# The low-rank gate product stacked in f32r, another pace for the gated linear attention, and a last product that is token-major

## The chip, the cores and the metric

One core of a Trainium2 chip runs the whole program in one launch. The metric is the device time of one execution in microseconds (us), the median of several runs. Before the change it is 1217.9 us (3 runs, 1216.07 to 1218.35).

## What is computed

Two blocks on one sequence of 512 tokens with 1024 features. The first is a hybrid mixer (pooling, two convolutions, differential attention) with a feed-forward net. The second puts 16 meta tokens in front (528 tokens in all) and has two layers, "ab" and "cd". Layer ab has eight heads of sparse attention (an indexer scores all keys, the 128 best are kept) and four heads of gated linear attention (GLA). Layer cd has four heads of retention and eight heads of stick-breaking attention, an output product, the residual sum and a last norm. The change touches the GLA of layer ab and the end of layer cd:

```python
log_a = log_sigmoid(ba @ gate_w2 + gate_b) / 16       # ba: 16 columns per token, gate_w2: 16 x 256
bcum = cumsum(log_a, within chunks of 64 tokens)
q_t, k_t = q * exp(bcum), k * exp(-bcum)              # then chunked linear attention with a carried state
...
h = h + concat([oc, od]) @ w_out_cd                   # end of layer cd
return h[16:] * rsqrt(mean(h[16:]**2) + 1e-6) * final_g
```

All inputs and outputs are float32.

## The kernel before

**Layout.** Activations lie feature-major: `self.x[kt]` holds features 128 kt to 128 kt + 127 on the partitions and tokens along the free axis. A large product is made of three f32r products: each operand is split into a rounded part (`hhi`, `whi`) and the rest (`hlo`, `wlo`), and hi*hi, lo*hi and hi*lo are added in PSUM (`f_acc`, its matmul is L154). Weights come as one stream in the order of use: `weights` (L129) loads a unit of 512 KB into one of two `wraw` tiles on SP's queue, ScalarE rounds it (L139) and VectorE makes the rest (L140), into four `whi` and four `wlo` tiles.

**Order.** The program is written as foreground projections, and `f_acc` calls `tick` after each pair of weight blocks: 8 ticks in a projection over 528 tokens (48 matmuls). One tick advances the generator at the head of the list `bg` by one `yield`. `pipe` runs a staged piece of work as such a generator: one round of stages, then `pace` yields. `finish(x)` ticks until x is done. On top of this the Tile framework places each engine's instructions by priority and by its own model of time: `first()` raises the priority, `chain()` raises it most. On the chip each engine works its list strictly in that order.

**Layer ab.** After the indexer's four query projections comes a projection `bw` of 104 columns: 64 indexer keys, 16 columns `ba` (partitions 64 to 79), 8 indexer weights. Then `score` (L855, L856) and `choose` (16 rounds of MAX8 and MATCH_REPLACE8 per block of 128 queries, L873 and L874, on VectorE; the masks `mk` are L876) stand in the list of generators while `bqk` and `bv` are projected. Then `gla` sets up its factors in a `chain()` block: the gate product (L1064, plain fp32, 16 rows, `gw2` as stationary and `bw[64:80]` as moving operand), Abs (L1065), min (L1066), Exp and Ln, the scan over time (L1071) with a tile `reset` of ones and zeros, and exponentials and products up to L1092. `reset` is one of the two `tmp` tiles, loaded at this point by SP (L1058). `linear` then runs five items (16 meta tokens, four blocks of 128) through four stages at a pace of 4, with fp32 matmuls (L1146, L1149, L1169, L1171, L1124). After it stand the projections of `av` (4) and those of `dsa_cols(0)` (q, k, gate); `finish(gla)` follows, then the output gates of GLA and the sparse attention `dsa` (L982 to L1032), whose blocks need the masks `mk`.

**End of layer cd.** When all heads are done, the `od` part is split into `mixed` (L112, L113) and the last four weight units are kept. For each half of the tokens (256 columns) 8 output tiles are made by `add_out`: 12 f32r matmuls of 256 columns, the residual sum on VectorE (L304), square on ScalarE (L242, L245), sum of squares on VectorE (L247), the product with `final_g` on ScalarE (L1378). Then `norm` sums over partitions with fp32 matmuls (L262), makes the inverse root (L264, L212 to L219), spreads it over partitions by two more matmuls (L223) and a copy (L269); eight multiplications (L1385) and four DMAs (L1386) end the half. The output is feature-major and is transposed on the host.

`transpose` (L184) is a fp32 matmul against the identity.

Of the kernel before, what the change touches and what calls it, by code (L numbers as in the profile page):

```python
# [18 lines left out]
S = 512  # L19
M = 16  # L20
T = S + M
H2 = M + S // 2
D = 1024
# [24 lines left out]
COLS, NCOLS = _names((("g1", 8), ("g2", 8), ("ga", 8), ("gc", 8), ("gf", 8), ("pscale", 2), ("sconv", 6),  # L48
# [12 lines left out]
class Kern:  # L61
    def __init__(self, ctx, tc, io, dbg=None):
        self.tc, self.nc, self.io = tc, tc.nc, io
        self.dbg = dbg or {}
        E = ctx.enter_context
        self.hot = E(tc.tile_pool(name="hot", bufs=1))

        self.hot.tile([128, 32], F32, name="pad1")
        self.wp = E(tc.tile_pool(name="w", bufs=2))
        self.const = E(tc.tile_pool(name="const", bufs=1))  # L70
        self.big = E(tc.tile_pool(name="big", bufs=1))
        self.dram = E(tc.tile_pool(name="dram", bufs=1, space=DRAM))
        self.big.tile([128, 24], F32, name="pad2")
# [746 lines left out]
    def layer_ab(self, act, acc):  # L820
# [4 lines left out]
        with tc.tile_pool(name="ab", bufs=1, reuse_waits="tile") as p:  # L825
            F4 = lambda n, w=T: p.tile([128, 4, w], F32, name=n)
            gw2 = p.tile([128, 256], F32, name="gw2")[64:80]
            nc.sync.dma_start(gw2, self.io["gw2"])
# [70 lines left out]
            gla = self.gla(p, bqk, bv, bvm, bw, gw2)  # L899
# [152 lines left out]
    def gla(self, p, bqk, bv, bvm, bw, gw2):  # L1052
# [3 lines left out]
        with self.chain():  # L1056
            reset = self.tmp(p)
            nc.sync.dma_start(reset, self.io["csa"][:, CSA["reset"][0]:CSA["reset"][0] + T])  # L1058
            for f in range(2):
                gb = self.cols[:, COLS["gb"][0] + f:COLS["gb"][0] + f + 1]  # L1060
                t, t2 = ks2[:, f], eb[:, f]
                for k0, k1 in ALL:
                    ps = self.ch("a")[:, :k1 - k0]
                    nc.tensor.matmul(ps, lhsT=gw2[:, f * 128:f * 128 + 128], rhs=bw[64:80, k0:k1], start=True, stop=True)  # L1064
                    nc.scalar.activation(t[:, k0:k1], ps, AF.Abs, bias=gb)  # L1065
                    nc.vector.tensor_scalar(t2[:, k0:k1], ps, gb, 0.0, op0=OP.add, op1=OP.min)  # L1066
# [30 lines left out]
            def masked(a, ps, n, e):  # L1097
# [3 lines left out]
                        lambda t: att0[t % 2], masked, bqk, True)  # L1101

    def linear(self, p, q, k, kx, qs, ks, v, vm, decay, att, masked, out, meta):
# [93 lines left out]
        yield from self.pipe([scores, attend, norm, finish], items, 4)  # L1197
# [75 lines left out]
    def layer_cd(self, act, acc):  # L1273
# [3 lines left out]
        with tc.tile_pool(name="cd", bufs=1, reuse_waits="tile") as p:  # L1277
# [35 lines left out]
            with self.chain():  # L1313
# [35 lines left out]
                def masked(a, ps, n, e):  # L1349
# [3 lines left out]
                            lambda t: p.tile([128, 4, 128], F32, name="att", bufs=2), masked, cqk, False)  # L1353
# [15 lines left out]
            acc = self.newacc()  # L1369

            self.keep = True
            ws = [self.weights(4, 256) for _ in range(4)]
            for c0 in (M, M + 256):
                c = slice(c0, c0 + 256)

                def after(kt):
                    self.sumsq(kt, c0, c0 + 256, acc, nc.vector)
                    nc.scalar.mul(self.x[kt][:, c], self.x[kt][:, c], self.cols[:, COLS["gf"][0] + kt:COLS["gf"][0] + kt + 1])  # L1378

                self.add_out(mixed, ((c0, c0 + 256),), after, ws)  # L1380
                _, rb = self.norm(acc, False, (c0, c0 + 256))
                for i, (k0, k1) in enumerate(((0, 2), (2, 4), (4, 6), (6, 8))):
                    for kt in range(k0, k1):
                        x = self.x[kt][:, c]
                        nc.vector.tensor_tensor(out=x, in0=x, in1=rb[:, c], op=OP.mult)  # L1385
                    (nc.sync if i % 2 else nc.scalar).dma_start(self.io["out"][k0:k1].rearrange("k p t -> p k t")[:, :, c0 - M:c0 - M + 256], self.xs[:, k0:k1, c])  # L1386
# [101 lines left out]
def _arrays(a):  # L1488
# [11 lines left out]
    for n, v in (("g1", a["norm1_g"][0]), ("g2", a["norm2_g"][0]), ("ga", a["norm_g_2"][0]), ("gc", a["norm_g_2"][1]),  # L1500
                 ("gf", a["final_g_2"]), ("pscale", a["pool_scale"][0]), ("sconv", a["sconv_w"][0].T),
                 ("cw", a["conf_dw_w"][0].T), ("cb", a["conf_dw_b"][0]), ("lng", a["conf_ln_g"][0]),
                 ("lnb", a["conf_ln_b"][0]), ("gb", a["gla_gate_b_2"][0]), ("sub", np.tile(a["subln_g"][0], 2))):
        col(n, v)
    out["cols"] = cols
    out["rows"] = np.concatenate([a[n][0] for n in ("q_norm_g", "k_norm_g", "lam_q1", "lam_k1", "lam_q2", "lam_k2")])
    out["relb"] = np.concatenate([a["rel_bias"][ORDER1].T, a["rel_bias_2"][ORDER2].T], axis=0)
# [16 lines left out]
    def wout(w, k0, k1):  # L1524
        for c in range(0, D, 256):
            unit(w, k0, k1, c, c + 256)
# [51 lines left out]
    wout(a["w_out_cd_2"][0], 4, 8)  # L1578
# [4 lines left out]
_OUT = (KT, 128, S)  # L1583
# [15 lines left out]
```

## Time and profile before

| | us |
|---|---|
| median of 3 runs | 1217.9 (1216.07 to 1218.35) |
| the profiled execution | 1222.06 |
| its span, first to last instruction | 1220.3 |
| TensorE busy (PE) | 1195.1 (98%) |
| VectorE busy (DVE) | 809.1 (66%) |
| ScalarE busy (ACT) | 622.0 (51%) |
| mean granted TensorE clock | 0.991 |

A timeline row reads: start, duration, engine, line, operation, output tile, input tiles, partitions x elements, count, and in brackets the idle time of the engine before it with what ended it. The duration of a matmul includes its way through the array, so matmuls overlap in the rows; how fast they pass is read from the distance of two starts. PEld is the load of a stationary operand, SPq and ACTq are DMA issues. The granted clock is 1.00 at 2.4 GHz and 0.50 at 1.2 GHz.

### The profile page before, as it was taken

How to read it: one execution, taken by the hardware profiler on the slowest of the kernel's cores; microseconds unless marked ns; L12 is line 12 of the kernel's file. 1: busy time of each engine (PE TensorE's matmuls, PEld its weight loads, DVE VectorE, ACT ScalarE, POOL GpSimd, SP SyncE). 2: the span in 40 equal slices, each digit the busy share in tenths (PEclk: the TensorE clock that was granted, in tenths of full speed). 3: DMA queues.
4: the chain of work that ended last, by engine and by line, in shares of the span. 5: the costliest groups of instructions: out<-in, count | busy, mean ns of one | idle time of the engine just before them, and what ended most of it. 6: DMA issues, size and time to landing. Idle time of an engine off the chain costs nothing.

```text
span 1220.3 us, 18958 instructions
## 1 busy us (share of the span) xinstructions
PE 1195.1 (98%) x7234; PEld 1022.5 (84%) x7234; DVE 809.1 (66%) x1834; ACT 622.0 (51%) x1382; POOL 51.1 (4%) x77
## 2 busy tenths in 40 slices
PE   8989899999999999999999999999999999999996
PEld 6978788888888888888999899898899889876776
DVE  6899966444433444455799899666575576775775
ACT  6378656333323333344453345656563575575754
POOL 7000002000000000011000000000020000000000
PEclk9999999999999999999999999999999999999998
DMA  7422123223223332234221122222132213220122
GB/s 235 114 70 70 37 68 104 89 101 101 74 95 113 101 102 88 84 96 127 73 70 61 36 78 79 71 71 64 59 103 91 87 53 105 70 70 18 52 69 70
DMA packets 33308, 101.28 MB, mean 83 GB/s; under 512 B 4048, under 2 KB 6640, under 8 KB 33216
## 3 DMA queue, kind: packets, MB, share of 16 engines
q1 hardware_dynamic: 30528, 95.66, 24.6%
q0 software_dynamic: 880, 2.25, 0.7%
q10 hardware_dynamic: 1808, 2.16, 0.5%
q8 instruction: 57, 0.93, 0.3%
q14 instruction: 35, 0.29, 0.1%
HBM read 95.87 MB, written 3.10 MB: 81 GB/s over the span
## 4 chain that ended last, share of the span: by engine, by line
PE 86%; DVE 9%; ACT 3%; DMA 1%; issue 1%; SPq 0%; DVEq 0%; ACTq 0%
PE mm L154 68%; PE psb L184 3%; DVE wlo L140 2%; DVE y L605 2%; PE pso L1265 1%; DMA wraw<-in_w 1%; DVE sc L874 1%; PE pso L1018 1%; DVE m L873 1%; ACT whi L139 1%; PE psa L1146 1%; PE pso L1020 1%; PE pso L566 1%; PE mm L173 1%; DVE qk L749 1%
## 5 line engine op out<-in xcount | busy, mean ns | idle before, releaser
L154 PE MATMUL mm<-hhi,whi 128*128 128x512 f32 (+2 forms) x1280 | 432.8, 338 | 0.0
L154 PE MATMUL mm<-hlo,whi 128*128 128x512 f32 (+2 forms) x1280 | 427.5, 334 | 0.0
L154 PE MATMUL mm<-hhi,wlo 128*128 128x512 f32 (+2 forms) x1280 | 427.0, 334 | 0.0
L139 ACT CAST whi<-wraw 128x512 fp32r<-128x512 f32 x350 | 207.6, 595 | 328.4 <-PE mm L154 297.1
L140 DVE TENSOR_TENSOR wlo<-wraw,whi 128x512 fp32r<-128x512 f32 x350 | 233.9, 672 | 153.5 <-ACT whi L139 127.4
L154 PEld LDWEIGHTS mm<-hhi,whi 128*128 128x128 f32 x1280 | 242.4, 189 | 23.9 <-issue 2.2
L154 PEld LDWEIGHTS mm<-hlo,whi 128*128 128x128 f32 x1280 | 242.3, 189 | 21.8 <-issue 0.8
L154 PEld LDWEIGHTS mm<-hhi,wlo 128*128 128x128 f32 x1280 | 242.1, 189 | 21.8
L154 PE MATMUL mm<-mx,whi 128*128 128x512 f32 (+2 forms) x448 | 113.5, 342 | 3.5 <-ACT mx L112 3.3
L154 PEld LDWEIGHTS mm<-mx,whi 128*128 128x128 f32 x448 | 76.7, 192 | 15.7 <-ACT mx L112 4.1
L710 DVE TENSOR_TENSOR gu<-mm,rb 128x512 f32<-128x512 f32 x44 | 30.4, 691 | 68.8 <-PE mm L154 67.0
L154 PE MATMUL mm<-mx,wlo 128*128 128x512 f32 (+2 forms) x224 | 75.0, 335 | 0.0
L154 PE MATMUL mm<-hidh,wlo 128*128 128x512 f32 x176 | 68.5, 389 | 0.0
L154 PE MATMUL mm<-hidh,whi 128*128 128x512 f32 x176 | 68.5, 389 | 0.0
L154 PE MATMUL mm<-hidl,whi 128*128 128x512 f32 x176 | 68.5, 389 | 0.0
L247 POOL TENSOR_TENSOR acc<-acc,sq 128x528 f32<-128x528 f32 (+1 forms) x18 | 25.7, 1426 | 806.6 <-ACT sq L245 489.5
L316 DVE TENSOR_TENSOR tmp<-mm,rb 128x272 f32<-128x272 f32 (+2 forms) x76 | 35.6, 468 | 24.0 <-PE mm L154 22.8
L304 DVE TENSOR_TENSOR x<-x,mm 128x272 f32<-128x272 f32 (+2 forms) x72 | 36.7, 509 | 14.4 <-PE mm L154 13.2
L154 PEld LDWEIGHTS mm<-mx,wlo 128*128 128x128 f32 x224 | 42.8, 191 | 3.6
L605 DVE SCALAR_TENSOR_TENSOR y<-u,cols,y 128x512 f32<-128x512 f32 x60 | 42.5, 747 | 0.2
L154 PEld LDWEIGHTS mm<-hidh,wlo 128*128 128x128 f32 x176 | 33.0, 188 | 6.9
L154 PEld LDWEIGHTS mm<-hidh,whi 128*128 128x128 f32 x176 | 33.0, 188 | 6.9
(406 smaller groups left out, 1819.6 us busy)
## 6 DMA issues: line engine op xcount, KB each, us to landing
wraw<-in_w SPq DMA_DIRECT2D x145, 512.0 KB, 3.5
wraw<-in_w SPq DMA_DIRECT2D x16, 384.0 KB, 2.9
wraw<-in_w SPq DMA_DIRECT2D x16, 320.0 KB, 2.8
bh<-tab SPq DMA_DIRECT2D x16, 132.0 KB, 2.9
mx<-cqk SPq DMA_DIRECT2D x8, 132.0 KB, 2.4
x<-in_x SPq DMA_DIRECT2D x4, 256.0 KB, 7.3
x<-in_x ACTq DMA_DIRECT2D x4, 256.0 KB, 4.6
B<-tab POOLq DMA_DIRECT2D x4, 256.0 KB, 8.2
```

The source lines that it names most:

```text
L139: self.nc.scalar.copy(hi[:, :w], raw[:, c])
L140: self.lo.tensor_tensor(out=lo[:, :w], in0=raw[:, c], in1=hi[:, :w].bitcast(F32), op=OP.subtract)
L154: nc.tensor.matmul(ps[b], lhsT=ww[i][:, f0:f0 + nf], rhs=aa[:, t0:t1], start=first and i == 0 and j == 0, stop=last and i == n - 1 and j == 2)
L173: nc.tensor.matmul(part(t), lhsT=aa[:, t0:t0 + nt], rhs=ww[i], start=u + i + j == 0 and t % 2 == 0, stop=u == 1 and i == 3 and j == 2, ski ...
L184: self.nc.tensor.transpose(out, in_, self.ident[:n, :n])
L247: e.tensor_tensor(out=acc[:, c0:c1], in0=acc[:, c0:c1], in1=sq[:, c0:c1], op=OP.add)
L304: nc.vector.tensor_tensor(out=x, in0=x, in1=p, op=OP.add)
L316: self.nc.vector.tensor_tensor(out=out[:, t0:t1], in0=p, in1=rb[:nf, t0:t1], op=OP.mult)
L566: nc.tensor.matmul(o[:, h * 64:h * 64 + 64], lhsT=pT[:, j * 128:(j + 1) * 128], rhs=vt[:, j, h * 64:h * 64 + 64], start=j == 0, stop=j == i)
L605: nc.vector.scalar_tensor_tensor(y[:, f], u[:, f, k:k + S], cw[:, f, k:k + 1], y[:, f], op0=OP.mult, op1=OP.add)
L710: nc.vector.tensor_tensor(out=t[:, g], in0=ps, in1=rbx, op=OP.mult)
L749: nc.vector.tensor_tensor(out=ll[a:a + 64], in0=src, in1=hh[r:r + 64].bitcast(F32), op=OP.subtract)
```

## The change

1. The gate product is stacked: a tile `bs` of 80 rows holds the rounded `ba` on rows 0 to 15 and 64 to 79 and the rest on rows 32 to 47 (zeros between), `gw2` holds the rounded weights on rows 0 to 15 and 32 to 47 and their rest on rows 64 to 79. One f32r matmul with 80 rows gives the three partial products. `bs` takes a `qk` slot, the raw weights a `tmp` slot.
2. `reset` is a tile of its own, loaded at the start of layer ab.
3. `linear` runs GLA at a pace of 6; retention keeps 4.
4. The last product is token-major: for each block of 128 tokens and each half of the features, four transposes put the residual into a PSUM bank, and 12 f32r matmuls of 512 columns add to it. The square sum comes from ScalarE's `accum_out`, `final_g` is a row spread over partitions by DMA (`gf`, two `tmp` tiles), the inverse root is a column, and each half is stored by one DMA. The last four weight units have shape 2 x 512 in place of 4 x 256. `final_g` leaves the `cols` table (8 columns), and a pad tile grows by 8 columns.

```diff
-            gw2 = p.tile([128, 256], F32, name="gw2")[64:80]
-            nc.sync.dma_start(gw2, self.io["gw2"])
+            gw2 = p.tile([128, 256], F32R, name="gw2")[:80]
+            reset = p.tile([128, T], F32, name="reset")
+            nc.sync.dma_start(reset, self.io["csa"][:, CSA["reset"][0]:CSA["reset"][0] + T])
...
+            bs = p.tile([128, T], F32R, name="qk", bufs=self.nqk)[:80]
+            graw = self.tmp(p)[:80, :256]
+            with self.chain():
+                nc.gpsimd.memset(graw, 0.0)
+                for r in (0, 32, 64):
+                    nc.sync.dma_start(graw[r:r + 16], self.io["gw2"])
+                nc.scalar.copy(gw2, graw)
+                nc.vector.tensor_tensor(out=gw2[64:80], in0=graw[64:80], in1=gw2[64:80].bitcast(F32), op=OP.subtract)
+                nc.gpsimd.memset(bs.bitcast(F32), 0.0)
+                for r in (0, 64):
+                    nc.scalar.copy(bs[r:r + 16], bw[64:80])
+                nc.vector.tensor_tensor(out=bs[32:48], in0=bw[64:80], in1=bs[64:80].bitcast(F32), op=OP.subtract)
...
-            reset = self.tmp(p)
-            nc.sync.dma_start(reset, self.io["csa"][:, CSA["reset"][0]:CSA["reset"][0] + T])
...
-                    nc.tensor.matmul(ps, lhsT=gw2[:, f * 128:f * 128 + 128], rhs=bw[64:80, k0:k1], start=True, stop=True)
+                    nc.tensor.matmul(ps, lhsT=gw2[:, f * 128:f * 128 + 128], rhs=bs[:, k0:k1], start=True, stop=True)
...
-        yield from self.pipe([scores, attend, norm, finish], items, 4)
+        yield from self.pipe([scores, attend, norm, finish], items, pace)
...
-            ws = [self.weights(4, 256) for _ in range(4)]
-            for c0 in (M, M + 256):
-                c = slice(c0, c0 + 256)
-
-                def after(kt):
-                    self.sumsq(kt, c0, c0 + 256, acc, nc.vector)
-                    nc.scalar.mul(self.x[kt][:, c], self.x[kt][:, c], self.cols[:, COLS["gf"][0] + kt:COLS["gf"][0] + kt + 1])
-
-                self.add_out(mixed, ((c0, c0 + 256),), after, ws)
-                _, rb = self.norm(acc, False, (c0, c0 + 256))
-                for i, (k0, k1) in enumerate(((0, 2), (2, 4), (4, 6), (6, 8))):
-                    for kt in range(k0, k1):
-                        x = self.x[kt][:, c]
-                        nc.vector.tensor_tensor(out=x, in0=x, in1=rb[:, c], op=OP.mult)
-                    (nc.sync if i % 2 else nc.scalar).dma_start(...)
+            ws = [self.weights(2, 512) for _ in range(4)]
+            for t in range(4):
+                c = slice(M + 128 * t, M + 128 * t + 128)
+                ps = [self.ch("a") if t % 2 else self.mm() for _ in range(2)]
+                ss = p.tile([128, 2], F32, name="ss", bufs=2)
+                out = []
+                for half in range(2):
+                    for j in range(4):
+                        nc.tensor.matmul(ps[half][:, j * 128:(j + 1) * 128], lhsT=self.x[half * 4 + j][:, c], rhs=self.ident,
+                                         is_transpose=True, start=j == 0, stop=False, skip_group_check=True)
+                    for k in range(4):
+                        ah, al = mixed[k]
+                        wh, wl = (w[k % 2] for w in ws[half * 2 + k // 2])
+                        for j, (aa, ww) in enumerate(((ah, wh), (al, wh), (ah, wl))):
+                            nc.tensor.matmul(ps[half], lhsT=aa[:, c], rhs=ww[:, :512], start=False, stop=k == 3 and j == 2, skip_group_check=True)
+                    with self.first():
+                        sq = self.big.tile([128, T], F32, name="sq")
+                        nc.scalar.activation(sq[:, :512], ps[half], AF.Square, accum_out=ss[:, half:half + 1])
+                        out.append(p.tile([128, S], F32, name="L", bufs=5))
+                        if half == 0:
+                            nc.vector.tensor_scalar(ss[:, 0:1], ss[:, 0:1], 1.0 / D, EPS, op0=OP.mult, op1=OP.add)
+                            nc.vector.tensor_tensor(out=out[0], in0=ps[0], in1=gf[0], op=OP.mult)
+                with self.first():
+                    nc.vector.scalar_tensor_tensor(ss[:, 0:1], ss[:, 1:2], 1.0 / D, ss[:, 0:1], op0=OP.mult, op1=OP.add)
+                    self.rsqrt(ss[:, 1:2], ss[:, 0:1])
+                    nc.scalar.mul(out[0], out[0], ss[:, 1:2])
+                    nc.vector.scalar_tensor_tensor(out[1], ps[1], ss[:, 1:2], gf[1], op0=OP.mult, op1=OP.mult)
+                    for half, e in enumerate((nc.scalar, nc.sync)):
+                        e.dma_start(self.io["out"][t * 128:(t + 1) * 128, half * 512:(half + 1) * 512], out[half])
```

## Rows read from the trace of the kernel before

**Rows 1.** The page: busy time of each engine, and the chain that ended last by engine.

```profile
PE 1195.1 (98%) x7234; PEld 1022.5 (84%) x7234; DVE 809.1 (66%) x1834; ACT 622.0 (51%) x1382; POOL 51.1 (4%) x77
PE 86%; DVE 9%; ACT 3%; DMA 1%; issue 1%; SPq 0%; DVEq 0%; ACTq 0%
```

**Rows 2.** Timeline of PE alone around the gate product (L1064; each product leaves two records).

```profile
633.43 0.72 PE L1064 MATMUL psa<-qk,gw 16*128 16x272 f32 x2
634.08 0.38 PE L856 MATMUL psa<-qk 128*128 128x256 f32 x1
...
635.14 1.41 PE L1064 MATMUL psa<-qk,gw 16*128 16x256 f32 x4
636.48 0.39 PE L154 MATMUL mm<-hhi,whi 128*128 128x272 f32 x1
...
637.54 0.69 PE L1064 MATMUL psa<-qk,gw 16*128 16x256 f32 x2
638.16 0.54 PE L154 MATMUL mm<-hlo,whi 128*128 128x272 f32 x1
...
641.62 0.31 PE L154 MATMUL mm<-hlo,whi 128*128 128x256 f32 x1
```

**Rows 3.** Stretches of one us: PE, PEld, DVE, ACT and POOL busy (count of instructions), granted clock, DMA share, GB/s.

```profile
637.00:638.00 1.00, 1.00 (x7) 0.69 (x6) 0.90 (x3) 0.93 (x3) 0.00 (x0) 1.00 0.80 307
...
639.00:640.00 1.00, 1.00 (x6) 1.00 (x6) 0.28 (x1) 0.97 (x2) 0.00 (x0) 0.50 0.00 0
```

**Rows 4.** Timelines of SP, DVE and PE: the load of `reset`, the scan, the wait of PE for the end of the set-up; and DVE's longest idle time in this stage.

```profile
657.55 0.33 SPq L1058 DMA_DIRECT2D tmp<-in_csa x1
660.94 2.38 DVE L1071 TENSOR_TENSOR_SCAN mx<-tmp,mx 128x528 f32<-128x528 f32 x2
668.53 0.28 PE L184 MATMUL psb<-keep,mx 128*16 128x128 f32 x1 [1.03 <-ACT mx L1092]
641.01 0.44 DVE L316 TENSOR_TENSOR tmp<-mm,rb 128x272 f32<-128x272 f32 x1 [1.72 <-PE mm L154]
```

**Rows 5.** Stretches of 20 us, columns as in rows 3.

```profile
580.00:600.00 20.00, 20.00 (x137) 18.15 (x136) 11.96 (x22) 8.74 (x18) 0.00 (x0) 1.00 0.24 80
...
640.00:660.00 20.00, 19.62 (x155) 19.03 (x154) 18.17 (x56) 5.97 (x11) 0.00 (x0) 0.96 0.23 68
660.00:680.00 20.00, 18.97 (x171) 16.70 (x169) 18.63 (x48) 9.67 (x24) 0.00 (x0) 1.00 0.16 53
680.00:700.00 20.00, 20.00 (x166) 16.82 (x163) 17.26 (x57) 6.44 (x19) 0.00 (x0) 1.00 0.09 27
700.00:720.00 20.00, 20.00 (x163) 19.23 (x162) 18.97 (x54) 7.94 (x17) 0.00 (x0) 1.00 0.25 78
720.00:740.00 20.00, 18.82 (x151) 17.92 (x149) 19.85 (x49) 12.60 (x30) 0.00 (x0) 1.00 0.25 80
```

**Rows 6.** Groups by line and shape: count, busy us, mean ns, idle before.

```profile
L749 DVE TENSOR_TENSOR qk<-tmp,qk 64x528 fp32r<-64x528 f32 x32 | 22.4, 701 | 0.4
L540 ACT ACTIVATE e<-e,st 128x512 f32<-128x512 f32 x8 | 5.7, 718 | 0.0
L540 ACT ACTIVATION_READ_ACCUMULATOR e<-e,st 128x1 f32 x32 | 6.1, 190 | 0.0
L1095 POOL MEMSET att<- 128x512 f32 x2 | 1.0, 524 | 0.0
```

**Rows 7.** What SP's queue waited for: total us, times, longest; and the issue of the output's DMAs.

```profile
SPq L129 <- DVE wlo L140: 866.8, 153, 27.4
out<-x SPq DMA_DIRECT2D x4, 256.0 KB, 2.6
```

**Rows 8.** Timeline of PE: matmuls of 512 and of 256 columns, and groups of transposes between f32r matmuls.

```profile
1178.27 0.39 PE L154 MATMUL mm<-mx,wlo 128*128 128x512 f32 x1
...
1178.95 0.39 PE L154 MATMUL mm<-mx,wlo 128*128 128x512 f32 x1
...
1188.22 0.28 PE L154 MATMUL mm<-mx,hlo 128*128 128x256 f32 x1
...
1188.57 0.28 PE L154 MATMUL mm<-mx,hlo 128*128 128x256 f32 x1
...
658.09 0.79 PE L184 MATMUL psb<-keep,tmp 128*128 128x128 f32 x4
...
658.85 0.29 PE L154 MATMUL mm<-hhi,whi 128*128 128x272 f32 x1
...
696.63 0.60 PE L184 MATMUL psb<-keep,ot 128*128 128x128 f32 x4
...
697.18 0.28 PE L154 MATMUL mm<-hhi,wlo 128*128 128x256 f32 x1
```

**Rows 9.** Timeline of all engines at the end, from the first matmul of the last product.

```profile
1185.30 0.45 PE L154 MATMUL mm<-mx,hhi 128*128 128x256 f32 x2
...
1209.14 0.28 PE L154 MATMUL mm<-mx,hlo 128*128 128x256 f32 x1
...
1211.55 0.16 DVE L264 TENSOR_SCALAR rcv<-pso 128x2 f32<-128x2 f32 x1 [0.76 <-PE pso L262]
...
1212.60 0.16 DVE L219 SCALAR_TENSOR_TENSOR rc<-rt,ry 128x2 f32<-128x2 f32 x1
...
1213.94 2.77 DVE L1385 TENSOR_TENSOR x<-x,rb 128x256 f32<-128x256 f32 x8 [1.18 <-ACT rb L269]
```

More of the change, by code (lines that the diff above doesn't have):

```diff
@@ L72, in __init__ @@
         self.dram = E(tc.tile_pool(name="dram", bufs=1, space=DRAM))
-        self.big.tile([128, 24], F32, name="pad2")
+        self.big.tile([128, 32], F32, name="pad2")
         self.ps = E(tc.tile_pool(name="ps", bufs=1, space=PSUM))
@@ L898, in layer_ab @@
             self.finish(chosen)
-            gla = self.gla(p, bqk, bv, bvm, bw, gw2)
+            gla = self.gla(p, bqk, bv, bvm, bs, gw2, reset)
             self.bg.append(gla)
@@ L1050, in pipe, with gla @@
                 yield
-    def gla(self, p, bqk, bv, bvm, bw, gw2):
+    def gla(self, p, bqk, bv, bvm, bs, gw2, reset):
         nc = self.nc
@@ L1100, in gla, with linear @@
             return self.linear(p, bqk[:, 0:2], bqk[:, 2:4], ks, q2, ks2, bv, bvm, lambda f, t: dec[:, f, t:t + 1],
-                        lambda t: att0[t % 2], masked, bqk, True)
-    def linear(self, p, q, k, kx, qs, ks, v, vm, decay, att, masked, out, meta):
+                        lambda t: att0[t % 2], masked, bqk, True, 6)
+    def linear(self, p, q, k, kx, qs, ks, v, vm, decay, att, masked, out, meta, pace):
         nc = self.nc
@@ L1352, in layer_cd @@
                 ret = self.linear(p, cqk[:, 0:2], cqk[:, 2:4], None, qs, ks, cv, cvm, lambda f, t: dec[:, f:f + 1],
-                            lambda t: p.tile([128, 4, 128], F32, name="att", bufs=2), masked, cqk, False)
+                            lambda t: p.tile([128, 4, 128], F32, name="att", bufs=2), masked, cqk, False, 4)
             self.bg.append(ret)
@@ new lines, in layer_cd @@
+            for half in range(2):
+                gf.append(self.tmp(p)[:, :512])
+                g = self.io["gfr"]
+                nc.sync.dma_start(gf[half], bass.AP(tensor=g.tensor, offset=g.offset + half * 512, ap=[[0, 128], [1, 512]]))
+            self.keep = True
+            ws = [self.weights(2, 512) for _ in range(4)]
[4 more added lines that the diff above has]
+                out = []
+                for half in range(2):
+                    for j in range(4):
[20 more added lines that the diff above has]
+                        e.dma_start(self.io["out"][t * 128:(t + 1) * 128, half * 512:(half + 1) * 512], out[half])
@@ L1506, in _arrays @@
     out["rows"] = np.concatenate([a[n][0] for n in ("q_norm_g", "k_norm_g", "lam_q1", "lam_k1", "lam_q2", "lam_k2")])
+    out["gfr"] = a["final_g_2"]
     out["relb"] = np.concatenate([a["rel_bias"][ORDER1].T, a["rel_bias_2"][ORDER2].T], axis=0)
@@ L1577, in _arrays @@
     wout(a["w_out_cd_2"][0], 0, 4)
-    wout(a["w_out_cd_2"][0], 4, 8)
+    for c in (0, 512):
+        for k in (4, 6):
+            unit(a["w_out_cd_2"][0], k, k + 2, c, c + 512)
     out["w"] = np.concatenate(parts)
     return out
-_OUT = (KT, 128, S)
+_OUT = (S, D)
 def kernel(**inputs):
@@ L1597 @@
     r = _run(nc, [{f"in_{n}": a for n, a in arrays.items()}], core_ids=[0])
-    return np.ascontiguousarray(r.results[0]["out"].reshape(D, S).T)[None]
+    return np.ascontiguousarray(r.results[0]["out"])[None]
```

7 lines of the change are left out of this document (3 added, 4 removed).

## The prediction

> **What bounds the kernel now.** First the page: PE is busy 98% of the span and carries 86% of the chain that ended last [rows 1]. So a microsecond counts where PE's list gets shorter or where PE waits; work of the other engines counts only where PE ends up waiting for it. Then I looked, by the change's two places, at the timeline of PE, at the granted clock per microsecond, at DVE's share per 20 us, and at the end in the timeline of all engines.
>
> At the gate product (633 to 642 us) the reader sees three bursts of plain fp32 records with 16 rows [rows 2], and right behind them a stretch in which the clock reads 0.50, its lower level of 1.2 GHz, although PE was busy in every microsecond before [rows 3]. At 668.53 PE waits 1.03 us for the end of GLA's set-up; its scan began only at 660.94, and `reset` was loaded from 657.55 [rows 4]. From 700 on DVE is close to full (19.85 of 20 us in 720 to 740) [rows 5]. At the end, PE's last matmul starts at 1209.14, and 7.3 us of small dependent steps follow until the last multiplication ends at 1216.71 [rows 9].
>
> **The sum** is made against the profiled execution (1222.06 us, of which the span is 1220.3); the median of the runs is 4.2 us below it, and I take the difference over to the median.
>
> **1. Gate product.** Its fp32 records hold PE for 0.65 + 1.34 + 0.62 = 2.6 us (633.43 to 634.08, 635.14 to 636.48, 637.54 to 638.16) [rows 2]. Four f32r matmuls of about 264 columns come at the pace of the 256-column ones, three in 0.35 us [rows 8]; that is 4 x 0.12 = 0.5 us. 80 rows instead of 16 change nothing in this: the full f32r matmuls have 128. That gives -2.1. The first matmul behind each burst is slower too (0.39 us against 0.28 later), so up to -2.7; I take -2.4.
>
> **2. The clock.** From 638.16 to 641.62 PE runs 3.46 us at half speed [rows 2, 3]; at the upper level this work takes 1.73 us. Nothing but the 16-row fp32 records sets the time before it apart, and they go. I take -1.6; bounds 0 and -1.73.
>
> The Trainium skill, "TensorE: Matmul & The Clock Gate", section "Why this matters for your kernels", ties a loss of clock in mid-kernel to gaps in which the engine idles. The trace disagrees for this fall: PE shows 1.00 of each microsecond busy before it [rows 3]. By the page alone the fall is not the product's doing and would stay; that is rival B.
>
> **3. `reset` in its own tile.** The 264 KB load leaves SP's list at 657.55 and joins it near the start of the layer, where DVE and ACT have half their time free (580 to 600) [rows 5]. The scan no longer waits for a `tmp` slot and a landing and can come up to 18 us earlier. PE's 1.03 us [rows 4] goes: -1.0, bounds 0 and -1.03. SP loses one wait ahead of a weight load; PE did not wait for that load, so nothing.
>
> **4. New small work.** Two POOL memsets (0.52 us for 128x512 [rows 6]), three DMAs of 16 KB on SP, three ACT copies and two DVE subtractions of at most 0.70 us each [rows 6], all near 600 us. DVE's 11.96 and ACT's 8.74 of 20 us hide it [rows 5]. If the cover were gone: 2 x 0.70 on DVE, +1.4. I take 0. What stands behind a waiting copy on ACT is a weight cast, and PE waits for that; the case in which this bites is rival D.
>
> **5. Pace 6.** Eight rounds at 6 ticks are 48 ticks; the `av` projections and `dsa_cols(0)` offer 7 x 8 = 56, so GLA still ends under cover. Its matmuls stay the same in number, only the changes between fp32 and f32r are spread differently. 0, bounds -0.5 and +0.5.
>
> **6. What is late next.** Items 1 to 3 put PE 5.0 us ahead by 700. DVE has its 16 rounds of `choose` for the last two masks still to do there and must come along. In 640 to 720 it idles 80 - 73.0 = 7.0 us [rows 5]. 1.72 us of this is its wait for the slow PE at 641.01 [rows 4] and goes by itself; of the other 5.3, waits inside GLA's chain, I let half be filled, since the set-up moves in front of them. So DVE gains 4.3, and 0.7 of PE's lead is given back: net -4.3. Bounds: -1.7, if DVE gains only its wait for PE, and -5.5.
>
> **7. The last product on PE.** Now its matmuls start from 1185.30 to 1209.14, with one pitch of 0.117 more 23.96 us [rows 9]. After: 4 x 2 x 12 = 96 matmuls of 512 columns, three in 0.68 us [rows 8], are 21.8 us. To this come 8 groups of four transposes. Such a group delays the f32r stream by 697.18 - 696.63 - 0.117 = 0.43 us, or 658.85 - 658.09 - 0.125 = 0.64 us [rows 8]; I take 0.5, nearer to the group that waits for nothing, and 4.0 us in all. 25.8 - 23.96 = +1.8; bounds +1.3 and +2.9. The L304 sums, squares and multiplications by `final_g` go from DVE and ACT; PE didn't wait for them, nothing. PSUM: blocks alternate between two pairs of banks, each pair has some 6 us to be emptied.
>
> **8. The end.** From the end of the last matmul (1209.42) to the end of the last multiplication (1216.71) it takes 7.3 us [rows 9]. After: square with accumulation 0.72 and its read 0.19 [rows 6]; six small steps as today from L264 to L219, 1211.55 to 1212.76, 1.21 us [rows 9]; one DVE product with PSUM, 0.70 [rows 6], the ACT one beside it; hand-overs 0.1. Sum 2.9: -4.4, bounds -4.1 and -4.7. Then the stores: today 1216.71 to 1220.3, 3.6 us, with four stores of the last half under way; after, two. A store lands in 2.6 us [rows 7], so at best -1.0, at worst 0; I take -0.2. SP also loads two `gf` rows of 256 KB behind the last weights; they are wanted 3 us into the last product, so 0.
>
> Items 7 and 8: +1.8 - 4.4 - 0.2 = -2.8, bounds -4.4 and -1.2.
>
> **Sum:** -4.3 - 2.8 = -7.1. The profiled execution would be 1215.0, the median 1217.9 - 7.1 = 1210.8 us. All bounds together: -2.4 to -10.4, 1207.5 to 1215.5.
>
> **The rivals.**
> A. DVE is the bound from 700 to 767 and gives back all but 1.7 us. For it: 19.85 of 20 us [rows 5]. Against: 7 us of idle time just before. -1.7 - 2.8 = -4.5: 1213.4.
> B. The clock falls all the same. Then PE is only 3.4 ahead, which DVE can follow: -3.4 - 2.8 = -6.2: 1211.7.
> C. Transposes at 0.64 us, a slower end and no gain in the stores: -4.3 - 1.2 = -5.5: 1212.4.
> D. The slower side: SP. The three loads of `graw` wait for a POOL memset, and this for a `tmp` slot that an indexer projection must release. If they stand in SP's list ahead of a weight load, the stream is held behind them. SP's waits are otherwise only for freed `wraw` tiles (up to 27.4 us at a time [rows 7]), so it normally runs ahead; it turns into loss when the hold outlasts the two `wraw` tiles and the split units in hand. One projection of 48 matmuls at 0.125 (6.0 us), a landing (2.6) and a fall of the clock behind the gap (1.7) are +10.3: total +3.2, 1221.1.
> E. The planner's new lists eat the gain in waits that I can't name: no change, 1217.9.
> F. The clock falls in the last product. Against it: the transposes at 658.09 and 696.63 lie in stretches with 1.00 but for the fall of rows 3 [rows 5]. Two falls at 1.7 each: -3.7, 1214.2.
>
> For F the Trainium skill, same page, section "Part 4: PE-mode transpose", says that such a transpose "doesn't count as PE-busy the same way". No run yet shows 32 of them in 26 us.
>
> **Chances.** Forecast 0.46, A 0.17, B 0.10, C 0.08, D 0.08, E 0.08, F 0.03. The likeliest case has its own range of 1208 to 1213.5. For 8 in 10 I leave out D, half of E and the outermost of the forecast: 1207 to 1217. About 0.2% (2.4 us) is what a measurement tells from no change: faster means below 1215.5. Forecast, A, B and C nearly whole and most of F: 0.80. E and the upper tail of A and F: 0.12. D: 0.08.
>
> **What would show it.** Right: four f32r records with 80 rows, PE moving on within 0.15 us of each; the clock at 1.00 through 633 to 645; the scan 10 us or more ahead of where it was; no wait of PE for L1092; last matmul to last multiplication 2.9 us; the last product's matmuls 25.8 us from first to last. Wrong: PE waits for DVE or for casts that add up to over 2 us between 640 and 770 (A), or near 600 (D); a clock of 0.50 at the product (B) or after 1185 (F); groups of transposes over 0.6 us (C). The forecast fails as a whole if PE's lead at 700 is under 3 us or the end is shorter by less than 3 us.

## The result, and the profile after

The kernel after takes 1212.29 us (median of 4 runs, 1211.59 to 1212.49) against 1218.12 us (4 runs, 1216.07 to 1219.93): ratio 0.9947, 95% interval 0.9934 to 0.9960. The forecast was 1210.8 in a range of 1207 to 1217: 7.1 us less, where 5.8 were measured by the medians and 6.5 by the ratio. So sign and size came out, but several of the terms behind them did not, as the experiments show.

The page of the kernel after, engines and chain (as [rows 1]):

```profile
PE 1187.8 (98%) x7154; PEld 1015.4 (84%) x7154; DVE 799.7 (66%) x1808; ACT 619.1 (51%) x1375; POOL 51.9 (4%) x79
PE 88%; DVE 7%; ACT 3%; DMA 2%; issue 1%; SPq 0%; DVEq 0%; ACTq 0%
```

PE still bounds the kernel, now with 7.3 us less busy time. The product, in the timeline of PE (as [rows 2]):

```profile
632.84 0.29 PE L1077 MATMUL psa<-qk,gw 80*128 80x272 f32 x1
632.97 0.28 PE L871 MATMUL psa<-qk 128*128 128x256 f32 x1
...
633.76 0.39 PE L1077 MATMUL psa<-qk,gw 80*128 80x256 f32 x1
633.99 0.29 PE L154 MATMUL mm<-hhi,wlo 128*128 128x272 f32 x1
...
635.75 0.39 PE L1077 MATMUL psa<-qk,gw 80*128 80x272 f32 x1 [0.36 <-DVE mx L1079]
635.98 0.29 PE L154 MATMUL mm<-hhi,whi 128*128 128x272 f32 x1
...
636.36 0.29 PE L1077 MATMUL psa<-qk,gw 80*128 80x256 f32 x1
```

Four records with 80 rows in place of eight with 16; PE goes on 0.12 to 0.23 us after each. The third waits 0.36 us for DVE to empty a bank, which is new. The clock, in stretches of one us of PE (busy, granted clock, DMA share, GB/s), stays at its upper level where [rows 3] had 0.50:

```profile
637.00:638.00 1.00, 1.00 (x11) 1.00 0.60 229
638.00:639.00 1.00, 1.00 (x10) 1.00 0.05 20
639.00:640.00 1.00, 1.00 (x11) 1.00 0.00 0
```

GLA's set-up and start, from the timelines of DVE and PE (as [rows 4]): the scan stands at 637.39 and 641.25, not at 660.94, and the first scores at 655.70, not behind the wait at 668.53. That wait is gone.

```profile
637.39 1.25 DVE L1084 TENSOR_TENSOR_SCAN mx<-reset,mx 128x528 f32<-128x528 f32 x1
...
641.25 1.25 DVE L1084 TENSOR_TENSOR_SCAN mx<-reset,mx 128x528 f32<-128x528 f32 x1
```
```profile
655.70 0.27 PE L1159 MATMUL psa<-bqk 64*16 64x16 f32 x8
```

The last product and the end, PE and then all engines (as [rows 9]):

```profile
1177.92 0.60 PE L1397 MATMUL mm<-keep,x 128*128 128x128 f32 x4
```
```profile
1203.60 0.40 PE L1403 MATMUL psa<-hlo,mx 128*128 128x512 f32 x1
1204.10 0.60 ACT L1406 ACTIVATE sq<-psa 128x512 f32<-128x512 f32 x1 [2.61 <-PE psa L1403]
...
1205.87 0.16 DVE L219 SCALAR_TENSOR_TENSOR ss<-rt,ry 128x1 f32<-128x1 f32 x1
1206.06 0.72 ACT L1414 ACTIVATE L<-L,ss 128x512 f32<-128x512 f32 x1 [0.61 <-DVE ss L219]
1206.13 0.75 DVE L1415 SCALAR_TENSOR_TENSOR L<-psa,ss,tmp 128x512 f32<-128x512 f32 x1
```

First to last matmul 25.7 us from start to start, and 25.9 with one more pitch, as the forecast of 25.8 counts it; end of the last matmul (1204.00) to the end of the last multiplication (1206.88) 2.9 us (forecast 2.9); from there to the end of the span (1210.7) 3.8 us, where it was 3.6.

**Where the time went.** The spans of the two profiled executions differ by 9.6 us, the medians by 5.8. To keep chance apart I count PE's records of the weight stream (lines 154 and 173), whose number is the same in all kernels up to the last product, and take the starts of the 2701st, 2781st and 4001st: 627.6, 643.6 and 883.9 us in the kernel before. Ahead of the first mark the change has only its small loads and copies; the stretch behind it holds the product, the third stretch the gated linear attention (GLA) and the sparse attention beside it, the last all the rest with the end. Differences to the profiled execution of before, in us, with the ratio of the runs:

```
kernel                    ratio (95%)            to 627.6  product  GLA    rest
after                     0.9947 (.9934-.9960)   -0.5      -3.5     -3.4   -2.2
after, once more          0.9944 (.9924-.9965)   -4.7      -3.5     -0.6*  -2.2
before + product          0.9959 (.9943-.9975)   -1.2      -3.5     -0.6   -0.1
before + end              0.9967 (.9951-.9984)   -0.8      -1.5     +0.2   -2.2
before + reset            0.9969 (.9952-.9985)   -3.7      -1.5     -3.9   +0.1
before + pace 6           0.9980 (.9965-.9996)   -3.3      -1.5     -2.3   +0.3
after - product           0.9931 (.9908-.9955)   -4.3      -1.5     -5.5   -2.4
after - reset             0.9954 (.9938-.9971)   -0.9      -3.5     -0.7   -2.4
after - pace              0.9915 (.9893-.9938)   -3.2      -3.5     -4.4   -2.2
after - pace, pairs kept  0.9903 (.9881-.9925)   -0.3      -3.4     -4.8   -4.8
after - pace, pairs split 0.9937 (.9912-.9962)   +1.2      -3.5     -2.6   -2.2
before, pairs kept        0.9986 (.9970-1.0001)  -1.5       0.0     -2.3   -0.4
before, product 4 times   1.0068 (1.0046-1.0090) -2.2      +9.6     -3.2   +0.5
* with two falls of the clock in this stretch (below)
```

The first column is chance. The differences in it, up to 5.9 us between two kernels, all arise before 160 us, in code that is the same everywhere. PE waits there for an ACT stage (L498: 3.1 us in the profile of before, 0.2 with `reset` alone), and behind this idle time the clock falls (at 68.2 us in before) or doesn't. The seven other profiles with a fall at 66 to 68 us stand between -1.5 and +1.2 in this column, the six without one between -4.7 and -2.2. The other columns are steadier: where the code of a stretch is the same and no fall of the clock lies in it, a profile differs from that of before by 0.2 us (GLA, with the end alone) and by at most 0.5 (the rest, with the old end). Mean clock and time go together in a kernel's own runs too: of the 33 runs of before beside the first four experiments, the 9 with a mean clock of 0.987 to 0.989 took 1223.3 us on average and the 8 with 0.994 or 0.995 took 1217.5.

Where the text below says what a group of PE's records adds up to, it counts each record from its start to the start of the next one, without the waits of PE.

### The profile page after: what moved, and what is told of

Its sections match the earlier page's. It is cut to its first block, busy times and chain, and to the rows that moved or that the text cites. A ratio compares the mean times of both kernels' runs of the same rounds, so it can differ in the third digit from the quotient of the medians.

```text
span 1210.7 us, 18780 instructions
## 1 busy us (share of the span) xinstructions
PE 1187.8 (98%) x7154; PEld 1015.4 (84%) x7154; DVE 799.7 (66%) x1808; ACT 619.1 (51%) x1375; POOL 51.9 (4%) x79
## 4 chain that ended last, share of the span: by engine, by line
PE 88%; DVE 7%; ACT 3%; DMA 2%; issue 1%; SPq 0%; DVEq 0%; ACTq 0%
PE mm L154 68%; PE psb L184 4%; DMA wraw<-in_w 2%; DVE y L605 2%; DVE wlo L140 1%; PE pso L1278 1%; PE pso L1033 1%; PE psa L1403 1%; PE mm L1403 1%; PE psa L154 1%; ACT whi L139 1%; PE pso L1035 1%; PE pso L566 1%; DVE sc L889 1%; PE psa L1252 1%
## 5 line engine op out<-in xcount | busy, mean ns | idle before, releaser
L154 PE MATMUL mm<-hhi,whi 128*128 128x512 f32 (+2 forms) x1280 | 432.8, 338 | 0.0
L154 PE MATMUL mm<-hlo,whi 128*128 128x512 f32 (+2 forms) x1280 | 426.0, 333 | 0.0
L154 PE MATMUL mm<-hhi,wlo 128*128 128x512 f32 (+2 forms) x1280 | 425.9, 333 | 0.0
L154 PEld LDWEIGHTS mm<-hhi,whi 128*128 128x128 f32 x1280 | 241.8, 189 | 23.9 <-issue 2.0
L154 PEld LDWEIGHTS mm<-hhi,wlo 128*128 128x128 f32 x1280 | 241.3, 189 | 21.8 <-issue 0.3
L154 PEld LDWEIGHTS mm<-hlo,whi 128*128 128x128 f32 x1280 | 241.5, 189 | 21.1 <-issue 0.2
L154 PE MATMUL mm<-mx,whi 128*128 128x512 f32 (+2 forms) x448 | 112.5, 340 | 4.0 <-ACT mx L112 3.3
L154 PEld LDWEIGHTS mm<-mx,whi 128*128 128x128 f32 x448 | 76.2, 190 | 15.7 <-ACT mx L112 4.2
L154 PE MATMUL mm<-mx,wlo 128*128 128x512 f32 (+2 forms) x224 | 74.7, 334 | 0.0
L154 PE MATMUL mm<-hidh,whi 128*128 128x512 f32 x176 | 68.5, 389 | 0.0
L154 PE MATMUL mm<-hidl,whi 128*128 128x512 f32 x176 | 68.5, 389 | 0.0
L154 PE MATMUL mm<-hidh,wlo 128*128 128x512 f32 x176 | 68.5, 389 | 0.0
L316 DVE TENSOR_TENSOR tmp<-mm,rb 128x272 f32<-128x272 f32 (+2 forms) x76 | 35.6, 469 | 25.9 <-PE mm L154 25.2
L154 PEld LDWEIGHTS mm<-mx,wlo 128*128 128x128 f32 x224 | 42.7, 191 | 3.5
L154 PEld LDWEIGHTS mm<-hidh,whi 128*128 128x128 f32 x176 | 33.0, 188 | 6.9
L154 PEld LDWEIGHTS mm<-hidl,whi 128*128 128x128 f32 x176 | 33.0, 188 | 6.9
L154 PEld LDWEIGHTS mm<-hidh,wlo 128*128 128x128 f32 x176 | 33.0, 188 | 6.8
```

Of the source, the lines that this page charges most:

```text
L154: nc.tensor.matmul(ps[b], lhsT=ww[i][:, f0:f0 + nf], rhs=aa[:, t0:t1], start=first and i == 0 and j == 0, stop=last and i == n - 1 and j == 2)
L316: self.nc.vector.tensor_tensor(out=out[:, t0:t1], in0=p, in1=rb[:nf, t0:t1], op=OP.mult)
```

## The experiments

**Each part alone.** The four parts of the diff, each put into the kernel before by itself, on one chip.

The product alone (`gw2`, `bs` and the f32r matmul; `reset` in `tmp`, pace 4, old end):

> The kernel before with the stacked f32r gate product alone (reset stays in tmp, pace 4, old end). My theory: the product takes 2.1 to 2.7 us less on PE and the fall of the clock to 0.50 behind it goes as well, 1.7 us; in the two profiles of before and after PE gained 3.4 us over this stretch together. DVE follows. Time 2.4 to 4 us below before: about 1214.5. PE's wait for GLA's set-up at the first scores stays, of the order of 1 us, since reset is still loaded late. Rival A (DVE is the bound from 700 on): the lead is there at 645 and half of it is gone by 770, time 1 to 2 us below. Rival B (the fall has another cause): a clock of 0.50 stays somewhere in 630 to 645, time about 2 us below. Rival D (SP held behind the loads of graw): 1 us or more slower than before.

Measured: median 1216.43 us, ratio 0.9959. The product's stretch is 3.5 us shorter, 1.5 of it because the clock does not fall here as it did in the profile of before, and the lead is kept. The wait for GLA's set-up, which `reset` still holds up, is there as expected (1.2 us, for DVE's L1093). B and D don't show.

The end alone (the hunk behind `mixed` in the last layer, with its weights and output layout):

> The kernel before with the token-major last product and norm alone. My theory: PE's last product takes 1.8 to 1.9 us longer (8 groups of four transposes, 25.9 us from the first to the last matmul in place of 24.0), the chain from the last matmul to the last multiplication falls from 7.3 to 2.9 us, and the stores give nothing: 2.2 to 2.8 us below before, about 1215.5, with nothing changed ahead of 1180 us. Rival C (transposes dear, end slower): 1.2 us below. Rival F (the clock falls in the last product): 0 to 1 us below, a clock of 0.50 after 1180.

Measured: 1216.70 us, ratio 0.9967; -2.2 us from 883.9 on. My theory holds, C and F don't: first to last matmul 1183.22 to 1208.90, 25.7 us, clock 1.00. One thing was not expected: this kernel has the old product, and yet its stretch is 1.5 us shorter than in the profile of before. The clock did not fall behind it.

`reset` alone:

```diff
+            reset = p.tile([128, T], F32, name="reset")
+            nc.sync.dma_start(reset, self.io["csa"][...])
...
-            reset = self.tmp(p)
-            nc.sync.dma_start(reset, self.io["csa"][...])
```

> The kernel before with reset in a tile of its own alone, loaded near 560 us. My theory: GLA's scan moves 10 us or more ahead and PE's wait of 1.03 us for the end of GLA's set-up goes; 0.5 to 1.0 us below before, and DVE's work of GLA moves ahead of its choose rounds. A second reading of the two profiles: because PE gained 4.4 us more between 640 and 715 than by the product, reset with the pace gives several us by filling DVE's idle time: then 2 to 4 us below. Rival: DVE is the bound afterwards and takes the wait back: within 0.3 us of before.

Measured: 1217.78 us, ratio 0.9969, and in the trace -3.9 us in the stretch of GLA. The second reading is right in size, but not in its reason: PE's waits in this stretch fall only from 3.5 to 2.8 us, because the wait of 1.03 us goes and smaller ones come. The rest is PE's own records. The products of q with the state take 1.7 us less, the products ahead of them 0.4 and the scores 1.0, as shown below; the second scores (L1149) take 0.4 more. The weight stream (L154) takes 0.8 us less: its first matmul behind any other record takes 0.22 us, one behind its own kind 0.125, and PE comes back to the stream 87 times instead of 94.

The pace alone (`..., bqk, True, 6)`, the retention at 4):

> The kernel before with the pace of six ticks in the gated linear attention alone. My theory: between 0.5 us below and 0.5 us above before. The other reading: it is the pace that lets PE run without waits in 640 to 715, 2 to 4 us below. Rival: with reset still late, the slower pace moves the end of GLA behind its cover and the time is 1 us or more above before.

Measured: 1218.30 us, ratio 0.9980; -2.3 us in the stretch of GLA. So the forecast of no change fails, and the other reading is right in size but not in its reason: PE's wait of 1.0 us for the set-up (L1092) is still there, and its waits in the stretch fall by 0.2 us only. This gain too lies in PE's own records: 0.9 us in GLA's scores and products with the state, 0.6 in the weight stream and 0.7 in the sparse attention's lines and the transposes, where single lines move both ways. No run tells these apart.

The parts do not add up. By the ratios, the four alone give 5.0, 4.0, 3.8 and 2.4 us, 15.2 together, where the whole change gives 6.5. In the stretches, without the fall of the clock, they give 2.0, 2.2, 3.9 and 2.3, and the whole gives 7.6.

**Each part taken back.** The kernel after, and with one part undone.

> The kernel after, once more, beside the three kernels that each take one part back. 0.45 to 0.65% below before. In the records of the profiles so far the change consists of: the product 2.0 us shorter on PE; the reset in an own tile, by which GLA's scores and its products with the state stand in pairs of half the array and GLA's matmuls take some 3 us less in all, and a wait of 1 us goes; the end 2.2 us shorter.

Measured: 1212.80 us, ratio 0.9944, the same as the first time. Its profile has two falls of the clock in the stretch of GLA, at 659.8 and 724.7 us, which cost 2.8 us of the weight stream there. Ahead of the first PE was busy; the second follows two waits of 0.4 and 0.7 us.

> The kernel after with the old plain fp32 product of 16 rows. My theory: PE stands 1.9 to 2.4 us longer at the product, and the clock falls behind it in every execution: 3.5 us above the kernel after, a clock of 0.50 at 630 to 645. Rival B: the fall at 638 in the profile of before came by chance, for the profiles with the end, the reset or the pace alone keep the old product and show no fall there: 2.0 us above the kernel after, no fall in the profile.

Measured: 1212.36 us, ratio 0.9931: not slower than the kernel after. Neither theory foresaw it. The product's stretch is 2.0 us longer, as B said, with no fall; but GLA's is 2.0 us shorter. What PE waited for between 640 and 770 us (total, times, longest), first in the kernel after, then without the product:

```profile
PE psb L184 <- ACT em L1007: 0.7, 1, 0.7
PE psb L184 <- ACT bv L794: 0.7, 1, 0.7
PE psb L184 <- DVE S L1146: 0.6, 1, 0.6
PE psa L997 <- DVE nm L1001: 0.4, 1, 0.4
PE pso L1035 <- DVE pT L1021: 0.4, 1, 0.4
PE pso L1033 <- DVE ag L1047: 0.3, 1, 0.3
```
```profile
PE psb L184 <- ACT em L994: 1.0, 1, 1.0
PE psb L184 <- DVE S L1133: 0.6, 1, 0.6
PE psb L184 <- ACT bv L794: 0.2, 1, 0.2
PE psa L984 <- DVE nm L988: 0.2, 1, 0.2
```

That is 3.1 us of waits with the new product and 2.0 without: with it, PE comes earlier and stands longer, for ACT and DVE. This is 1.1 of the 2.0 us; over the whole stretch it is 1.0. The other 1.0 is the weight stream's, to which PE comes back 87 times instead of 93; the sparse attention's lines, whose order also changed, move both ways by up to 0.8 us.

> The kernel after with reset loaded late into tmp. My theory (only PE's wait of 1.03 us comes back): 0.5 to 1.0 us above the kernel after. The other theory (by the early reset GLA starts 10 us sooner, and its matmuls then fall into an order in which two of 64 rows stand side by side and run together): the 32 products of q with the state take about 4.9 us instead of 3.2, the scores 3.9 instead of 2.8, and the time is 3 to 4.5 us above the kernel after, or 2 to 3 if the pace of six still brings one of the four tiles into that order.

Measured: 1214.54 us, ratio 0.9954, and 2.7 us more than the kernel after in the stretch of GLA: the other theory, in its weaker form. The runs themselves are only 1.2 (by the ratios) to 1.7 us (by the medians) above the kernel after, with overlapping intervals. From start to start of the next record the 32 products of q with the state add up to 4.4 us (3.2 in the kernel after, 4.9 before), the scores to 3.8 (2.8 and 3.9).

> The kernel after with the pace of four in GLA. My theory: within 0.5 us of the kernel after. The other theory (the order of GLA's matmuls decides): reset alone had three of four tiles in pairs, as the kernel after has, so again within 0.5 us; if the order comes out differently, up to 2.5 us above, and then the time of the 32 products with the state goes from 3.2 towards 4.9 us. Rival A (DVE decides from 700 on): GLA's work comes sooner at pace four and pushes choose back, 1 us or more above.

Measured: 1209.00 us, ratio 0.9915: 3.8 us lower than the kernel after beside it, though the intervals of the two ratios overlap. None of the three readings foresaw a gain. In the trace it is 1.0 us ahead in the stretch of GLA. GLA's scores and products with the state take what they took at pace six (2.8 and 3.2 us), so their order is not the reason. PE's waits are 0.3 us shorter, with those for `pT` and `ag` gone, and the sparse attention's scores and products (L997, L998, L1033) 0.8 us. Against before, pace six gave 2.3 us by itself; beside the early `reset` it costs about 1.0 in the trace.

**The order of the records.** Timeline of PE in the kernel before, one tile of GLA (L1171 is the product of q with the state, bank by bank):

```profile
676.56 0.71 PE L1171 MATMUL psb<-S,mx 64*128 64x128 f32 x4
677.11 0.61 PE L1146 MATMUL psa<-bqk 64*128 64x128 f32 x4
...
678.90 0.71 PE L1171 MATMUL pso<-S,mx 64*128 64x128 f32 x4
679.54 0.33 PE L1124 MATMUL psb<-bv,kst 128*64 128x128 f32 x2
```

and the same product in the kernel after:

```profile
669.36 0.37 PE L1184 MATMUL pso<-S,mx 64*128 64x128 f32 x1
669.36 0.37 PE L1184 MATMUL psb<-S,mx 64*128 64x128 f32 x1
669.57 0.27 PE L1184 MATMUL pso<-S,mx 64*128 64x128 f32 x1
669.58 0.27 PE L1184 MATMUL psb<-S,mx 64*128 64x128 f32 x1
...
669.79 0.27 PE L1184 MATMUL pso<-S,mx 64*128 64x128 f32 x1
669.80 0.27 PE L1184 MATMUL psb<-S,mx 64*128 64x128 f32 x1
670.00 0.55 PE L1137 MATMUL psb<-bv,kst 128*64 128x128 f32 x6
```

Before, bank `psb` (rows 64 to 127 of the array) takes 0.55 us for its four records and bank `pso` (rows 0 to 63) 0.64, at two different times: 1.19 us. After, the two banks alternate, each second record starts 0.01 us after its partner, and all eight take 0.64 us. Three of GLA's four tiles stand so after, none before. The program writes them alternating in both kernels, and the planner orders them otherwise in some tiles. Why the early `reset` changes its order is not shown; that it splits the pairs where one bank comes free before the other is a guess. The Trainium skill, "TensorEngine Tiling (Array Packing)", section "Tiling Modes", says that tiles of the array operate independently, and section "Restrictions and Gotchas" that different row tiles cannot use one PSUM bank at the same time; the trace agrees with the first (0.01 us between partners) and uses two banks throughout. Three kernels test whether the order decides. In the first, L1157, L1182 and L1184 stand pinned to the written order in both linear attentions:

```diff
-                            nc.tensor.matmul(o, lhsT=qs[...], rhs=st[...], ...)
+                            ins = nc.tensor.matmul(o, lhsT=qs[...], rhs=st[...], ...)
+                        if (inter or f or e):
+                            self.tc.keep_in_program_order(ins)
```

> The kernel after with pace four, and the eight products of a tile (attend) and the scores of both linear attentions pinned to their written order, in which rows 0 to 63 and rows 64 to 127 of the array alternate. If it is the alternation that makes them cheap: the one GLA tile that is not yet in pairs saves 0.6 us, two tiles of the retention 0.6 us each, some scores up to 1 us: 1.5 to 2.5 us below the kernel with pace four alone, the records of the second product with the state in pairs 0.01 us apart in all eight tiles. Rival: the pin makes PE wait for the second bank and costs what it saves: within 1 us of the kernel with pace four.

Measured: 1208.24 us, ratio 0.9903, the lowest of all, but the runs do not tell it from pace four alone (0.9915, with overlapping intervals); the stretches do. Its trace is 0.3 us ahead of that kernel in GLA's stretch and 2.5 us in the rest, where the retention runs. All 32 products with the state now take 2.6 us in each attention, and all stand in pairs; the retention had 3.4, and its scores and first products take 1.0 and 0.6 us less. That is 2.3 of the 2.5 us. GLA's scores lost 0.4 us again.

The second writes GLA's scores and products bank by bank:

```diff
+            if meta:
+                order.sort(key=lambda i: i[2])
```

> The kernel after with pace four, and GLA's scores and products written bank by bank, so that four records with the same 64 rows follow each other; start and set-up of GLA as early as with pace four. If the order decides: 0.64 us in each of the three tiles that were in pairs, and up to 0.45 us in each of four tiles of scores: 2 to 3.7 us above the kernel with pace four, nearly all of what the early reset gave. Rival (the early scan itself gives the time, by filling DVE and by the wait that goes): within 0.5 us of the kernel with pace four.

Measured: 1212.02 us, ratio 0.9937; 1.9 us more in the stretch of GLA than with pace four, while its set-up is as early. By the ratios it is 2.7 us above that kernel, with overlapping intervals. The 32 products take 5.1 us instead of 3.2, and the products ahead of them (L1183) 5.8 instead of 5.2. The scores did not change (2.8): the planner put them back in pairs, 0.01 us apart, so this run tests the products alone. One tile in its timeline:

```profile
674.78 0.71 PE L1183 MATMUL pso<-bv,att 128*128 128x128 f32 x4
675.42 0.71 PE L1185 MATMUL pso<-S,mx 64*128 64x128 f32 x4
676.06 0.71 PE L1183 MATMUL psb<-bv,att 128*128 128x128 f32 x4
676.70 0.71 PE L1185 MATMUL psb<-S,mx 64*128 64x128 f32 x4
```

The third pins GLA alone in the kernel before, `reset` still late:

> The kernel before, with reset still late, and only GLA's scores and products pinned to alternate. If the order decides: four tiles at 0.64 us and some of the scores, 2.5 to 3.5 us below before, with PE's wait of 1.0 us for GLA's set-up still there. Rival (the early scan gives the time): within 0.5 us of before, or above it by the waits of PE for the second bank.

Measured: ratio 0.9986, its interval reaching to 1.0001; in the trace -2.3 us in the stretch of GLA, with the wait of 1.0 us for L1092 still there and a wait for DVE (L986) that grew from 0.4 to 1.1 us. The 32 products take 2.6 us instead of 4.9, the products ahead of them 0.4 less and the scores 0.2 less. So in PE's records the order alone saves 3.0 us, without the early `reset`; the stretch keeps 2.3 of it, a little under the forecast, and the runs are too scattered to say that it reaches the end.

**The clock behind the product.** Of the six profiles with the old product at its place two have a fall behind it (before, and before with pairs kept, at 636.8), of the seven with the new one none. That alone could be chance. The last run makes the suspected cause bigger:

```diff
-                    nc.tensor.matmul(ps, lhsT=gw2[...], rhs=bw[64:80, k0:k1], start=True, stop=True)
+                    for _ in range(4):
+                        nc.tensor.matmul(ps, lhsT=gw2[...], rhs=bw[64:80, k0:k1], start=True, stop=True)
```

> The kernel before with each matmul of the old gate product (plain fp32, 16 rows) issued four times over, which gives the same result and 7.8 us more of these records. If they are what makes the clock fall behind them: a clock of 0.50 between 630 and 660 in the profile, in all executions and not in two of six as so far, and 7.8 us on PE plus 1.2 us for the rarer falls of before: 9 us or more above before. If the falls there come by chance: clock 1.00 through the stretch in the profile, and 6 to 8 us above before.

Measured: 1227.60 us, ratio 1.0068 (8.3 us; 7.1 by the medians). The products in its timeline, then stretches of PE (busy, granted clock, DMA share, GB/s):

```profile
631.25 2.10 PE L1065 MATMUL psa<-qk,gw 16*128 16x272 f32 x8
634.33 9.64 PE L1065 MATMUL psa<-qk,gw 16*128 16x256 f32 x24
```
```profile
632.00:634.00 2.00, 2.00 (x12) 1.00 0.00 0
634.00:636.00 2.00, 2.00 (x11) 0.89 0.71 238
636.00:638.00 2.00, 2.00 (x6) 0.50 0.10 33
...
646.00:648.00 2.00, 2.00 (x11) 0.50 0.00 0
648.00:650.00 2.00, 2.00 (x14) 0.69 0.00 0
```

The clock is at 1.2 GHz from 635.6 to 649.3 us with PE busy throughout, and all six runs have a mean clock of 0.982 to 0.989 (before beside them 0.988 to 0.995). The one profile has the fall, and the mean clocks fit one in each of the six runs. So a long stretch of these records does bring the clock down. That the product issued once does so in some executions fits two profiles of six; whether it is the 16 rows or the plain fp32 is not separated. The time is under the 9 us that the theory asked for: the stretch is 9.6 us longer in the trace, but GLA's takes 3.2 of it back.

## Why the prediction was right, and where it was not

**1, the gate product: right, a little less.** -2.4 was forecast, -2.0 measured (15.9 - 1.5 of the fall - 12.5). The term mis-sized is the new product at 0.5 us: its four records hold PE for 0.71, two of them for 0.23 where my sign allowed 0.15, and 0.36 us of wait for L1079 comes on top.

**2, the clock: cause supported, size wrong.** The -1.6 took one profile for every execution. With two falls in six, of 1.5 us each, it is worth about 0.5 us on average, an estimate. Rival B, by which the clock falls all the same, did not come in seven profiles with the new product, and the run with the product four times speaks for the product as the cause.

**3, `reset`: the step that failed.** The scan and the wait came as forecast, but "-1.0, bounds 0 and -1.03" priced only the wait. `reset` alone gave 3.9 us in the trace: the tiles of GLA then fall into pairs (3.1 us in the scores and products), PE comes back to the weight stream less often (0.8), and PE's waits fall by 0.7 in all, not by 1.03. Some lines lost 0.7 us. I had counted the matmuls as "the same in number" (item 5) and never asked at what pitch they run in another order.

**4, the new small work: right at 0.** PE kept its place to 0.1 us between 528 and 610 us. D did not come: SP issued the loads of `graw` at 583.6 and the weight load behind them at 587.2.

**5, the pace: failed.** "0, bounds -0.5 and +0.5" is -2.3 alone and about +1.0 beside the other parts. Alone, 0.9 us is the reason of 3, the order of GLA's records. Beside the other parts that order is the same at both paces, and the +1.0 lies in the sparse attention's records and in PE's waits. This is E's premise, lists of the planner that decide, with both signs.

**6, what is late next: the giving back came, but not by the wait for DVE that I priced.** I let DVE give back 0.7 of 5.0. PE's lead over the profile of before held from 719 to 755 us (8.4 and 8.3) and lost 1.0 by 840. PE's waits in that stretch are 0.4 us in both kernels; the 1.0 is the weight stream's (0.9, with 39 returns to it instead of 34) and L1033's (0.4, the line L1018 of before). A's own sign did not come either: PE's waits for DVE between 640 and 770 add up to 1.7 us, and with those for ACT to 3.1, where before had 3.3. Yet of the product's 2.0 us nothing is left in the whole kernel: the kernel without it is 2.0 us faster in the stretch of GLA and not slower in its runs. About half of that is longer waits for ACT and DVE, as A's mechanism would have it for one part, and half the weight stream's records. Whether it is so whatever the order of the records stays open: the product alone kept its gain.

**7 and 8, the end: right.** Forecast +1.8, -4.4 and -0.2. Measured, from first to last start, 25.7 - 23.8 = +1.8, then 2.9 - 7.3 = -4.4, and the stores +0.2 instead; with 0.1 for the longer last matmul, -2.2 against -2.8. The term mis-sized is the stores. C did not come (96 matmuls at 0.233 leave 0.4 us for a group of transposes), nor F (clock 1.00 through the last product, with 32 transposes in 26 us).

In sum items 1 to 6 gave -6.9 in the trace, or -5.4 without the fall of the clock, where the forecast of -4.3 counted 1.6 for this fall; the end gave -2.2, forecast -2.8. That the forecast stood near the result is in part luck: the pairs, which it did not have, stood in for the clock and for the product's lost gain.

## What to carry to other kernels

When an edit moves work in a kernel that a planner orders, count the matmuls by pitch as well as by number: products of 64 rows cost about half when partners with the other 64 rows and another bank stand right behind them (0.64 us for eight, 1.2 to 1.3 bank by bank), and the planner may part them. Pinning the written order kept all products with the state in pairs here, whatever the rest of the timing, at a price of 0.4 us in GLA's scores; with the pace of four it is the lowest time of the study, by a margin that the runs do not resolve. And compare stage by stage, from a mark before the change: a difference of spans of one execution each held up to 5.9 us of chance here.

## What the hardware showed that was not expected

Half-array matmuls into two banks start 0.01 us apart, and eight take the time of four (0.64 us). The clock can fall with PE busy: within the old product, four times over, for 13.7 us; and in the second profile of the kernel after right behind GLA's first tile, whose records have 16 and 64 rows:

```profile
656.62 0.39 PE L1182 MATMUL pso<-bvm,att 16*16 16x128 f32 x2
...
657.59 0.65 PE L1137 MATMUL psb<-bvm,kst 16*64 16x128 f32 x8
658.17 0.71 PE L1159 MATMUL psa<-bqk 64*128 64x128 f32 x8
658.82 0.45 PE L1162 MATMUL psa<-bqk,mx 64*64 64x64 f32 x8
...
660.17 0.42 PE L154 MATMUL mm<-hhi,wlo 128*128 128x256 f32 x1
```

There the 256-column pitch goes from 0.12 to 0.21 us until 663.1. That tile stands in every kernel of the study; the fall behind it in one profile only.
